# Two more weight-block sums of each seven-product pair made by adding DMAs, with the first two sums' signs turned

## The chip, the cores and the metric

The kernel runs on one core of a Trainium2 chip. The metric is the device time of one execution in microseconds; a version's time is the median of its runs. A profiled execution gives the trace, whose times count from the first instruction.

## The reference

A trunk of two layers on 256 positions with a model width of 2048, all in fp32. The first layer is a gated MLP whose positions are mixed in chunks of 128, the second is stick-breaking attention with 16 heads of 128. Each layer normalizes its input, multiplies it with a wide weight matrix, mixes, gates, and multiplies with an output matrix; the result is added to the residual.

```python
def reference(x, norm_g, a_w_in, a_v_norm_g, a_w_s, a_b_s, a_w_out, b_w_in, b_w_out, final_g):
    h = x
    for i in range(DEPTH):
        hn = rms_norm(h, norm_g[i])
        j = i // N_MIXERS
        if i % N_MIXERS == 0:
            y = gmlp_branch(hn, a_w_in[j], a_v_norm_g[j], a_w_s[j], a_b_s[j], a_w_out[j])
        else:
            y = stick_breaking_branch(hn, b_w_in[j], b_w_out[j])
        h = h + y
    return rms_norm(h, final_g)
...
def gmlp_branch(xn, w_in, v_g, w_s, b_s, w_out):
    proj = xn @ w_in                       # 2048 x 12288: u | v | gate
    ...
    y = u * mixed * jax.nn.silu(zg)
    return y @ w_out                       # 4096 x 2048
...
def stick_breaking_branch(xn, w_in, w_out):
    proj = xn @ w_in                       # 2048 x 8192: q | k | v | gate
    ...
    o = o.reshape(B, S, SB_WIDTH) * jax.nn.silu(zg)
    return o @ w_out                       # 2048 x 2048
```

## The kernel before

**Splitting.** Each fp32 operand is split into a high part `hi` and a remainder `lo`, and a product is made of three matmuls (`terms`, lines 119 to 121: hi·hi, lo·hi, hi·lo). For weights this is done by `cut` (lines 114 and 115): ScalarE casts a block of 128x1024 into `hi`, VectorE subtracts to make `lo`. Five pairs of such buffers exist (`wspl`), so the splitting can run ahead of TensorE by five blocks.

**Pairs.** The weights are read in column blocks of 512 (`CB`). Two column blocks are worked on together, as a `Pair`. There are 22 pairs in the program: three of the v projection (named v2, v4, v6 after their column block), eight gu (gate and u of one block), two o, four qk, two bv, two bg, and one f2. For a part of the rows (`HALVES`, four or five row blocks of 128 in each half, `ks`) the pair uses a scheme of seven block products in place of eight (Strassen's, in a form of Winograd's). The left operand is split into two position tiles (`a11`, `a12` belong to the first 128 positions, `a21`, `a22` to the second), the right operand into blocks `b11`, `b12`, `b21`, `b22` (first digit: half of the rows, second digit: column block). It needs four sums of the left side (s1 to s4: made once for each operand by `Left.sums`, `fifth` or `sums_of`) and four sums of weight blocks, made for each pair:

- b12 - b11, multiplied with s1 (product p5)
- b22 + (b12 - b11), multiplied with s2 (p6)
- b12 + b22, multiplied with s3 (p7)
- b21 less the second sum, multiplied with a22 (p4)

Every group of two row blocks is one tile of 128x1024 (0.524 MB); with five row blocks there is a third group of one row block, 128x512. Groups 0 and 1 live in `sraw`, one buffer for each of the eight tags; a third group of b21 and b22 is loaded into `wraw` by `others`.

**How the sums are made before.** In `head`, b11 is multiplied (p1), then `minus` (lines 284 to 286) overwrites b11 with b12 - b11 on VectorE, and `plus` (lines 288 to 294) lets an adding DMA, issued by POOL, add block (1, 1), which is b22, into b12. After p5, line 314 adds b22 into b11 on VectorE for the groups 0 and 1; a third group gets its addition from an adding DMA. In `body`, p6 uses b11; p2 uses b21; p7 uses b12; then line 339 calls `minus` once more for b21 - b11 into b11, for all groups; p3 uses b22 and p4 uses b11.

**Order.** The bank `a` holds p1, then also p2; `e` holds p5. A copy of `e` in SBUF (`es`, line 328) is added to the banks `b` (line 334) and `c` (line 342). After p4 come `mid` (the pair's own work: gains or position mixing) and `column(0)`: the remaining rows, in raw blocks of two row blocks, three buffers (`wraw`), multiplied in the plain way. `column(1)` is kept back as `tail` and its steps are put between the blocks of the next pair's p1, p5 and p6 (`run`).

**Queues.** SyncE issues the plain loads (line 223). POOL issues the adding DMAs; their list is `adds`. The loads of the gains `vg` (line 527) and of the mixing matrices `ws` (line 597) are issued by POOL after `adds[-1]`, the last add so far; `ws` then gets a triangular selection on POOL (line 602), a cast on ScalarE (line 604) and a subtract on VectorE (line 605). Each engine works through its own queue in order; the order within it is laid down when the program is built, by a simulated timeline and a few ordering constraints.

Of the kernel before, what the change touches and what calls it, by code (L numbers as in the profile page):

```python
# [11 lines left out]
AF = mybir.ActivationFunctionType  # L12
# [17 lines left out]
def trunk_kernel(ctx: ExitStack, tc: tile.TileContext, x, xt, gcols, wst, a_w_in, a_v_norm_g,  # L30
# [11 lines left out]
    nc = tc.nc  # L42
# [45 lines left out]
    def f(ap):  # L88
        return ap.bitcast(F32)
# [33 lines left out]
    class Left:  # L123
# [10 lines left out]
        def sums(self, ks, out, name):  # L134

            for k0 in range(0, ks, 4):
                n = min(4, ks - k0)
                full = []
                for i in range(2):
                    sl = slice(i * ks + k0, i * ks + k0 + n)  # L140
                    fl = sraw.tile([P, 4, S], F32, tag=f"b1{i + 1}_1", name=f"{name}_full{i}{k0}")
                    nc.vector.tensor_add(fl[:, 0:n], f(self.hi[:, sl, :]), f(self.lo[:, sl, :]))
                    full.append(fl)
                a11, a12 = full[0][:, 0:n, 0:P], full[1][:, 0:n, 0:P]
                a21, a22 = full[0][:, 0:n, P:S], full[1][:, 0:n, P:S]
                sm = [sraw.tile([P, 2, 4, P], F32, tag=f"b2{i + 1}_1", name=f"{name}_sm{i}{k0}") for i in range(2)]
                s1, s2, s3, s4 = sm[0][:, 0, 0:n], sm[0][:, 1, 0:n], sm[1][:, 0, 0:n], sm[1][:, 1, 0:n]
                nc.vector.tensor_sub(s1, a21, a22)
                nc.vector.tensor_sub(s3, a21, a11)
                nc.vector.tensor_sub(s2, a11, s1)  # L150
                nc.vector.tensor_sub(s4, a12, s2)
                for i, si in enumerate((s1, s2, s3, s4)):
                    o = out[:, :, i, k0:k0 + n]
                    nc.scalar.copy(o[:, 0], si)
                    nc.vector.tensor_sub(o[:, 1], si, f(o[:, 0]))
            self.s, self.ks = [out], ks

        def fifth(self, out, name):

            full = jk.tile([P, 2, S], F32, tag="sg0", bufs=1, name=f"{name}_full")  # L160
            sm = jk.tile([P, 4, P], F32, tag="sg1", bufs=1, name=f"{name}_sm")
            for i in range(2):
                for t in range(NT):
                    hi, lo = self.part(HALVES[i][4], t)
                    nc.vector.tensor_add(full[:, i, t * P:(t + 1) * P], f(hi), f(lo))
            a11, a12, a21, a22 = full[:, 0, 0:P], full[:, 1, 0:P], full[:, 0, P:S], full[:, 1, P:S]
            nc.vector.tensor_sub(sm[:, 0], a21, a22)
            nc.vector.tensor_sub(sm[:, 1], a11, sm[:, 0])
            nc.vector.tensor_sub(sm[:, 2], a21, a11)
            nc.vector.tensor_sub(sm[:, 3], a12, sm[:, 1])  # L170
            nc.scalar.copy(out[:, 0, :, 0], sm)
            nc.vector.tensor_sub(out[:, 1, :, 0], sm, f(out[:, 0, :, 0]))
            self.s.append(out)

        def sums_of(self, y, ks, out, name):

            a11, a12 = y[0][:, :, 0:P], y[1][:, :, 0:P]
            a21, a22 = y[0][:, :, P:S], y[1][:, :, P:S]
            s13, s24 = (jk.tile([P, ks, P], F32, tag=f"sg{i}", bufs=1, name=f"{name}_{i}") for i in range(2))

            def split(i, si):
                o = out[:, :, i, 0:ks]
                nc.scalar.copy(o[:, 0], si)
                nc.vector.tensor_sub(o[:, 1], si, f(o[:, 0]))
            nc.vector.tensor_sub(s13, a21, a22)
            nc.vector.tensor_sub(s24, a11, s13)
            split(0, s13)
            split(1, s24)
            nc.vector.tensor_sub(s13, a21, a11)
            nc.vector.tensor_sub(s24, a12, s24)  # L190
            split(2, s13)
            split(3, s24)
            self.s, self.ks = [out], ks
# [39 lines left out]
    class Pair:  # L233
# [47 lines left out]
                tick(1)  # L281
                yield

        def minus(self, into, b0, b1, order=None):
            for g in order or range(len(self.groups)):
                nc.vector.tensor_sub(into[g], b0[g], b1[g])  # L286

        def plus(self, into, i, j, g0=0):

            for g in self.early:  # L290
                if g < g0:
                    continue
                k, n = self.groups[g]
                adds.append(nc.gpsimd.dma_start(into[g], self.src(HALVES[i][k], n, j), accum_op=ALU.add))  # L294

        def head(self):
            left = self.left
            self.b11 = self.load(0, 0)
            late = chain and self.name == "v2"
            if not late:  # L300
                self.b12 = self.load(0, 1)
            self.a = self.bank("a")
            for g, _ in enumerate(self.block(self.b11, lambda k: left.part(HALVES[0][k], 0), self.a, "p1", True)):
                yield
                if late and g == 0:
                    self.b12 = self.load(0, 1)
            self.b22 = self.load(1, 1)
            self.minus(self.b11, self.b12, self.b11, self.early)
            self.plus(self.b12, 1, 1)
            self.e = self.bank("e")  # L310
            yield from self.block(self.b11, lambda k: left.sum_part(0, k), self.e, "p5", True)
            self.b21 = self.load(1, 0)
            for g in range(len(self.b22)):
                nc.vector.tensor_add(self.b11[g], self.b22[g], self.b11[g])  # L314
            self.plus(self.b11, 1, 1, len(self.b22))

        def body(self, between=lambda: None):
            left = self.left
            b11, b12, b22, b21 = self.b11, self.b12, self.b22, self.b21

            def block(*args):
                for _ in self.block(*args):
                    between()
            a, e = self.a, self.e
            b = self.bank("b")
            nc.scalar.copy(b, a)
            es = jk.tile([P, CB], F32, tag="es", bufs=1, name=f"{self.name}_es")
            nc.scalar.copy(es, e)
            block(b11, lambda k: left.sum_part(1, k), b, "p6")
            c = self.bank("c")  # L330
            nc.scalar.copy(c, b)
            self.others(b21, 0)
            block(b21, lambda k: left.part(HALVES[1][k], 0), a, "p2")
            self.last_dve = nc.vector.tensor_add(b, b, es)
            self.others(b22, 1)
            block(b12, lambda k: left.sum_part(2, k), c, "p7")
            d = self.bank("d")
            self.last_act = nc.scalar.copy(d, c)
            self.minus(b11, b21, b11)
            block(b22, lambda k: left.sum_part(3, k), b, "p3")  # L340
            block(b11, lambda k: left.part(HALVES[1][k], 1), d, "p4")
            nc.vector.tensor_add(c, c, es)
            self.banks = ((a, d), (b, c))
            if self.mid is not None:
                self.mid(self)
            for _ in self.column(0):
                pass
# [239 lines left out]
    with ExitStack() as lg:  # L587
# [35 lines left out]
        def evac_gu(b, j, t, bank):  # L623
            y = v_of(t, b * CB, CB)
            sg = jk.tile([P, CB], F32, tag=f"sg{t}", bufs=1, name=f"{'gu'[j]}{b}_{t}")
            nc.scalar.activation(sg, bank, (AF.Silu, AF.Gelu_apprx_tanh)[j], scale=r1[:, t:t + 1])
            if j == 0:
                nc.vector.tensor_mul(y, y, sg)
            else:

                queue.append((1, lambda: times(y, sg)))

        def mid_gu(b, pair):
            nonlocal rv
            if rv is None:
                rv = rstd(1, NV, W, "nv")
                for i in (NV - 2, NV - 1):
                    gain(i, pair)
            mixing(b, pair)
            if b == NV - 1:  # L640
                drain()
                flush(make_yTs(0, "xs", "yc0"))
                for k2 in (12, 13):
                    make_yT(k2, yc3(k2))

        for b in range(NV):
            run(Pair(columns(a_w_in, 2 * W + b * CB, b * CB), left, KD, f"gu{b}", KS_GU[b],
                     lambda j, t, bank, b=b: evac_gu(b, j, t, bank), mid=lambda pair, b=b: mid_gu(b, pair), fifth_first=True))
# [120 lines left out]
    def plain(c, ks, before=None):  # L769
        return product(block_of(a_w_out, c * CB, CB), yl0, ks, f"op{c}", lambda t, bank: add_h(c, t, bank), before)  # L770
# [22 lines left out]
    g = plain(0, rest[16:20] + rest[:16] + rest[20:], beside_o0)  # L793
# [9 lines left out]
    g = plain(1, rest)  # L803
# [388 lines left out]
```

## Time and profile before

| what | value |
|---|---|
| median of 3 runs | 1144.99 us (1144.73 to 1146.62) |
| profiled execution, first to last instruction | 1142.0 us |
| its own time outside that span | not recorded; the median stands 3.0 us above the span |
| mean granted TensorE clock | 0.999 |
| TensorE busy | 1132.3 us (99%) |
| VectorE busy | 1010.9 us (89%) |
| ScalarE busy | 828.5 us (73%) |
| POOL busy | 99.8 us (9%) |
| moved by DMA | 264.72 MB, mean 232 GB/s |
| DMA issues by SyncE's and ScalarE's queues, share of 16 engines | 58.9% and 0.8% |
| DMA issues by POOL, share of 16 engines | 16.2% |

How to read the views: in the timeline a row has its start and its duration in us, the engine, the line, the operation, and out<-in by the program's names (without the number of the pair or the buffer). In brackets stands how long the engine was idle before it, and what ended that. L12 is line 12 of the kernel before. In a window's row stand the window and its length, each engine's busy time with its number of instructions, the granted clock, the mean busy share of the 16 DMA engines and the rate. Packets of different queues overlap, so that this share can pass 1. In the list of waits stand the time in all, how often, and the longest.

### The profile page before, as it was taken

What the parts mean: (1) busy time and instruction counts of PE and PEld (TensorE: products, weight loads), DVE (VectorE), ACT (ScalarE), POOL (GpSimd) and SP (SyncE); (2) the same over time, 40 slices, a digit from 0 to 9 for tenths busy, and PEclk for the clock granted to TensorE, in tenths of its full rate; (3) what the DMA queues carried; (4) which work ended last, traced back from release to release, by engine and by line L of the source; (5) the groups of instructions that cost most, each with busy time, mean ns of one, the idle gap of its engine ahead of it and who ended that gap; (6) DMA issues with size and microseconds to landing.
All of it is one profiled execution on the core that took longest, in us unless ns stands there. A gap on an engine that the chain in (4) does not pass through costs nothing.

```text
span 1142.0 us, 14838 instructions
## 1 busy us (share of the span) xinstructions
PE 1132.3 (99%) x5168; PEld 937.6 (82%) x5168; DVE 1010.9 (89%) x1111; ACT 828.5 (73%) x1102; POOL 99.8 (9%) x106
## 2 busy tenths in 40 slices
PE   9999999999999999999999999999999999999997
PEld 6788888888888888888888888888888888888886
DVE  7899889988998999978988678989889989897996
ACT  8776777777777778866657456788678887886564
POOL 0100110110110210100010001110100101100000
PEclk9999999999999999999999999999999999999999
DMA  9988788787797797685885868687687776837972
GB/s 335 317 290 270 214 252 270 194 266 241 173 274 249 191 261 240 177 296 142 267 259 166 276 203 282 153 280 211 181 283 200 211 230 174 272 88 241 325 225 92
DMA packets 135659, 264.72 MB, mean 232 GB/s; under 512 B 8992, under 2 KB 9504, under 8 KB 135456
## 3 DMA queue, kind: packets, MB, share of 16 engines
q1 hardware_dynamic: 117472, 227.57, 58.9%
q0 software_dynamic: 16304, 33.04, 16.2%
q10 hardware_dynamic: 1808, 3.17, 0.8%
q8 instruction: 40, 0.66, 0.2%
q14 instruction: 35, 0.29, 0.1%
HBM read 259.55 MB, written 4.19 MB: 231 GB/s over the span
## 4 chain that ended last, share of the span: by engine, by line
PE 93%; DMA 2%; DVE 2%; issue 1%; ACT 1%; SPq 0%; POOLq 0%; POOL 0%; ACTq 0%; DVEq 0%
PE gu_a L119 3%; PE gu_b L119 3%; PE gu_b L121 3%; PE gu_a L121 3%; PE gu_a L120 3%; PE gu_b L120 3%; PE op_acc L119 2%; PE op_acc L120 2%; PE op_acc L121 2%; PE gu_d L119 2%; PE gu_d L121 2%; PE gu_c L121 2%; PE gu_d L120 2%; PE gu_c L119 2%; PE gu_c L120 2%; PE qk_a L121 1%
## 5 line engine op out<-in xcount | busy, mean ns | idle before, releaser
L114 ACT CAST gu_p_hi<-gu_b 128x1024 fp32r<-128x1024 f32 (+1 forms) x126 | 122.9, 1004 | 38.4 <-DVE gu_b L314 16.1
L115 DVE TENSOR_TENSOR gu_p_lo<-gu_b,gu_p_hi 128x1024 fp32r<-128x1024 f32 (+1 forms) x126 | 142.8, 1165 | 1.9 <-ACT gu_p_hi L114 1.2
L115 DVE TENSOR_TENSOR qk_p_lo<-qk_b,qk_p_hi 128x1024 fp32r<-128x1024 f32 (+1 forms) x77 | 80.8, 1073 | 8.9 <-ACT qk_p_hi L114 8.4
L114 ACT CAST qk_p_hi<-qk_b 128x1024 fp32r<-128x1024 f32 (+1 forms) x77 | 70.5, 934 | 19.0 <-DMA qk_b<-in_b_w_in 4.0
L115 DVE TENSOR_TENSOR gu_lo<-gu_raw,gu_hi 128x1024 fp32r<-128x1024 f32 x60 | 72.1, 1218 | 12.5 <-ACT gu_hi L114 12.2
L114 ACT CAST gu_hi<-gu_raw 128x1024 fp32r<-128x1024 f32 x60 | 62.0, 1052 | 21.0 <-DMA gu_raw<-in_a_w_in 11.5
L115 DVE TENSOR_TENSOR v_lo<-v_raw,v_hi 128x1024 fp32r<-128x1024 f32 (+1 forms) x41 | 48.9, 1193 | 15.2 <-ACT v_hi L114 15.2
L114 ACT CAST v_hi<-v_raw 128x1024 fp32r<-128x1024 f32 (+1 forms) x41 | 41.7, 1028 | 27.9 <-DMA v_raw<-in_a_w_in 26.4
L115 DVE TENSOR_TENSOR v_p_lo<-v_b,v_p_hi 128x1024 fp32r<-128x1024 f32 x42 | 50.3, 1220 | 3.3 <-ACT v_p_hi L114 3.1
L114 ACT CAST v_p_hi<-v_b 128x1024 fp32r<-128x1024 f32 x42 | 43.0, 1049 | 9.8 <-PE v_c L121 4.9
L115 DVE TENSOR_TENSOR bg_p_lo<-bg_b,bg_p_hi 128x1024 fp32r<-128x1024 f32 (+1 forms) x42 | 42.5, 1041 | 4.8 <-ACT bg_p_hi L114 4.7
L114 ACT CAST o_p_hi<-o_b 128x1024 fp32r<-128x1024 f32 (+1 forms) x35 | 33.4, 965 | 18.1 <-PE op_acc L121 13.0
L115 DVE TENSOR_TENSOR bv_p_lo<-bv_b,bv_p_hi 128x1024 fp32r<-128x1024 f32 (+1 forms) x42 | 42.5, 1040 | 3.8 <-ACT bv_p_hi L114 3.6
L114 ACT CAST bv_p_hi<-bv_b 128x1024 fp32r<-128x1024 f32 (+1 forms) x42 | 37.4, 908 | 10.0 <-DMA bv_b<-in_b_w_in 3.0
L294 POOL DMA_DIRECT2D gu_b<-in_a_w_in x20 | 23.0, 1155 | 240.2 <-DVE gu_b L286 134.3
L114 ACT CAST bg_p_hi<-bg_b 128x1024 fp32r<-128x1024 f32 (+1 forms) x42 | 37.3, 907 | 8.0 <-PE bg_a L121 2.5
L115 DVE TENSOR_TENSOR o_p_lo<-o_b,o_p_hi 128x1024 fp32r<-128x1024 f32 (+1 forms) x35 | 38.3, 1113 | 5.4 <-ACT o_p_hi L114 5.4
L286 DVE TENSOR_TENSOR gu_b<-gu_b,gu_b 128x1024 f32<-128x1024 f32 (+1 forms) x36 | 41.4, 1169 | 0.1
L114 ACT CAST o_hi<-o_raw 128x1024 fp32r<-128x1024 f32 x22 | 23.0, 1052 | 24.9 <-DMA o_raw<-in_a_w_out 24.8
L115 DVE TENSOR_TENSOR o_lo<-o_raw,o_hi 128x1024 fp32r<-128x1024 f32 x22 | 26.7, 1221 | 15.2 <-ACT o_hi L114 15.0
L114 ACT CAST op_hi<-op_raw 128x1024 fp32r<-128x1024 f32 x24 | 25.1, 1053 | 19.3 <-PE op_acc L121 8.8
L120 PE MATMUL op_acc<-op_lo,yc 128*128 128x512 f32 x96 | 37.8, 393 | 0.0
(798 smaller groups left out, 3797.8 us busy)
## 6 DMA issues: line engine op xcount, KB each, us to landing
gu_b<-in_a_w_in SPq DMA_DIRECT2D x64, 512.0 KB, 4.8
gu_raw<-in_a_w_in SPq DMA_DIRECT2D x60, 512.0 KB, 5.4
v_raw<-in_a_w_in SPq DMA_DIRECT2D x39, 512.0 KB, 5.5
qk_b<-in_b_w_in SPq DMA_DIRECT2D x32, 512.0 KB, 5.3
qk_raw<-in_b_w_in SPq DMA_DIRECT2D x26, 512.0 KB, 5.5
v_b<-in_a_w_in SPq DMA_DIRECT2D x24, 512.0 KB, 5.4
op_raw<-in_a_w_out SPq DMA_DIRECT2D x24, 512.0 KB, 4.9
o_raw<-in_a_w_out SPq DMA_DIRECT2D x22, 512.0 KB, 4.7
```

The lines of the kernel that those rows point to most:

```text
L114: nc.scalar.copy(hi[:, sl], raw[:, sl])
L115: low[0] = nc.vector.tensor_sub(lo[:, sl], raw[:, sl], f(hi[:, sl]))
L119: nc.tensor.matmul(acc, lh, hi, start=first, stop=False, skip_group_check=True)
L120: nc.tensor.matmul(acc, lh, lo, start=False, stop=False, skip_group_check=True)
L121: nc.tensor.matmul(acc, ll, hi, start=False, stop=last, skip_group_check=True)
L286: nc.vector.tensor_sub(into[g], b0[g], b1[g])
L294: adds.append(nc.gpsimd.dma_start(into[g], self.src(HALVES[i][k], n, j), accum_op=ALU.add))
```

## The change

Four things are changed, in all 22 pairs.

- The sum for p4: for the groups 0 and 1, `minus(b11, b21, b11)` on VectorE is gone. In its place, directly after p6, POOL issues `plus(b11, 1, 0, 0, 2)`: an adding DMA reads block (1, 0), which is b21, from HBM once more and adds it into b11. A third group keeps its subtract on VectorE.
- So that b21 only has to be added, the first two sums of the groups 0 and 1 are kept with the other sign: b11 gets b11 - b12 (a third group b12 - b11 as before), and line 314 subtracts b22 where it added it.
- The left sums match: in `sums` and `sums_of` s2 is turned (s1 - a11, and s4 = a12 + s2); in `fifth`, which serves the third group, s1 is turned (a22 - a21, and s2 = a11 + s1).
- p5 then comes out with the other sign, and the copy of `e` into `es` becomes an activation with scale -1.

The new adds are appended to `adds` as well, so that `vg` and `ws` are issued after them.

```diff
@@ Left.sums @@
-                nc.vector.tensor_sub(s2, a11, s1)
-                nc.vector.tensor_sub(s4, a12, s2)
+                nc.vector.tensor_sub(s2, s1, a11)
+                nc.vector.tensor_add(s4, a12, s2)
@@ Left.fifth @@
-            nc.vector.tensor_sub(sm[:, 0], a21, a22)
-            nc.vector.tensor_sub(sm[:, 1], a11, sm[:, 0])
+            nc.vector.tensor_sub(sm[:, 0], a22, a21)
+            nc.vector.tensor_add(sm[:, 1], a11, sm[:, 0])
@@ Left.sums_of @@
-            nc.vector.tensor_sub(s24, a11, s13)
+            nc.vector.tensor_sub(s24, s13, a11)
...
-            nc.vector.tensor_sub(s24, a12, s24)
+            nc.vector.tensor_add(s24, a12, s24)
@@ Pair @@
-        def minus(self, into, b0, b1, order=None):
-            for g in order or range(len(self.groups)):
-                nc.vector.tensor_sub(into[g], b0[g], b1[g])
-
-        def plus(self, into, i, j, g0=0):
+        def plus(self, into, i, j, g0=0, g1=9):
 
             for g in self.early:
-                if g < g0:
+                if not g0 <= g < g1:
                     continue
@@ head @@
-            self.minus(self.b11, self.b12, self.b11, self.early)
+            for g in self.early:
+                b = (self.b11[g], self.b12[g])[::1 if g < 2 else -1]
+                nc.vector.tensor_sub(self.b11[g], *b)
...
-                nc.vector.tensor_add(self.b11[g], self.b22[g], self.b11[g])
+                nc.vector.tensor_sub(self.b11[g], self.b11[g], self.b22[g])
@@ body @@
-            nc.scalar.copy(es, e)
+            nc.scalar.activation(es, e, AF.Identity, scale=-1.0)
             block(b11, lambda k: left.sum_part(1, k), b, "p6")
+            self.plus(b11, 1, 0, 0, 2)
...
-            self.minus(b11, b21, b11)
+            for g in range(2, len(self.groups)):
+                nc.vector.tensor_sub(b11[g], b21[g], b11[g])
```

## The prediction

> **What bounds the kernel now.** I read the page's busy times first, then the waits of TensorE, then windows over the span, and last the timeline of the first pair.
>
> ```profile
> span 1142.0 us, 14838 instructions
> PE 1132.3 (99%) x5168; PEld 937.6 (82%) x5168; DVE 1010.9 (89%) x1111; ACT 828.5 (73%) x1102; POOL 99.8 (9%) x106
> ```
>
> A busy TensorE isn't proof of one at its full rate, so the next two views are needed: what it waited for in the whole span, and how many matmuls it got through in windows with much and with little other work.
>
> ```profile
> PE wps L79 <- DVE warm L76: 1.3, 1, 1.3
> PE v_acc L120 <- DVE v_lo L115: 0.6, 1, 0.6
> PE gT L434 <- ACT bsg L1011: 0.2, 1, 0.2
> PE v_acc L119 <- ACT v_hi L114: 0.2, 1, 0.2
> ...
> 20.00:40.00 20.00, 19.44 (x86) 1.00 0.93 321
> 40.00:60.00 20.00, 20.00 (x90) 1.00 1.07 340
> 60.00:80.00 20.00, 19.86 (x88) 1.00 0.91 314
> 600.00:620.00 20.00, 20.00 (x94) 1.00 0.50 155
> 1080.00:1100.00 20.00, 20.00 (x90) 1.00 0.98 297
> 1120.00:1140.00 20.00, 14.76 (x66) 0.99 0.26 96
> ```
>
> Four waits, 2.3 us in all, three of them in the first 40 us (the loads and the first product, where the change does nothing). The windows (length, TensorE busy and its instructions, granted clock, DMA share, GB/s) show 90 matmuls in 20 us at a DMA share of 1.07 and 90 at 0.98; the 94 of the window with 0.50 hold short transposes. The clock is granted in full. So the rate of a matmul depends on nothing beside it, and from 40 us to the last product the only losses are the 0.14 us missing in 60:80 and the 0.2 us before gT. The change alters no matmul. TensorE sets the end, and what can be won is 0.34 us; the 7.2 us that it lacks in the last window and behind it belong to the final norm and the stores.
>
> **The change part by part.**
>
> (1) Removed: two subtracts into b11 in each pair (the groups 0 and 1; a group 2 keeps its own). One row holds all of line 286, then the queues' shares:
>
> ```profile
> 0.00:1142.00 1142.00, 120.52 (x110) 1.00 0.76 232
> q1 hardware_dynamic: 117472, 227.57, 58.9%
> q0 software_dynamic: 16304, 33.04, 16.2%
> ```
>
> 22 pairs run (v 3, gu 8, o 2, qk 4, bv 2, bg 2, f 1), so 44 of the 110 go, all of 128x1024. With 22 narrow ones at 0.68 us taken off, the 88 wide ones take 1.20 us each: 53 us leave VectorE, which falls from 1010.9 to some 958 us. That is worth the part of TensorE's waiting that VectorE caused after 40 us, which is none recorded. Its margin was thin in places:
>
> ```profile
> 438.24 3.48 DVE L115 TENSOR_TENSOR gu_p_lo<-gu_b,gu_p_hi 128x1024 fp32r<-128x1024 f32 x3
> 439.62 0.40 PE L120 MATMUL gu_b<-gu_p_lo,xs 128*128 128x512 f32 x1
> ```
>
> The first of the three subtracts ends near 439.45 and TensorE takes its result at 439.62. The change widens a margin of 0.17 us, but a margin isn't time: I count 0 us.
>
> (2) Added: 44 adding DMAs of 0.524 MB on POOL's queue, 23.1 MB. The software queue's 33.04 MB cost 16.2% of 1142 us, 185 us of all 16 engines, so 5.6 us per MB; the plain queue's 227.57 MB cost 673 us, 3.0 us per MB. The new work is 129 us, the share of the DMA engines rises from 0.76 to 0.87, and one pair gets 1.05 MB, 5.9 us. Whether that matters is read stage by stage. In a steady pair (gu1, the adds would run from about 217 to 227):
>
> ```profile
> 216.00:228.00 12.00, 12.00 (x55) 9.93 (x54) 11.72 (x12) 10.66 (x13) 1.14 (x1) 1.00 0.59 181
> 228.00:240.00 12.00, 12.00 (x55) 9.93 (x54) 9.10 (x11) 8.35 (x12) 0.00 (x0) 1.00 1.00 355
> 240.63 1.22 DVE L115 TENSOR_TENSOR gu_lo<-gu_raw,gu_hi 128x1024 fp32r<-128x1024 f32 x1
> 245.59 0.39 PE L120 MATMUL gu_a<-gu_lo,x_hi 128*128 128x512 f32 x1
> ```
>
> (Length, busy time of TensorE, of its weight loads, of VectorE, ScalarE and POOL, then clock, DMA share, GB/s.) From 216 to 228 the DMA engines are free for 0.41 x 12 = 4.9 us of the 5.9 needed. The last 1.0 us is pushed into the full stretch behind it. The raw block that is loaded at the end of that stretch is split by 241.85 and used at 245.59, a margin of 3.7 us that covers it: 0 us. With the cover gone, what the push has over 3.7 us would be lost in each such pair, at most 5.9 - 3.7 = 2.2 us, which only a hole filled by something else could bring about. I keep 0.7 us in all for the upper end.
>
> In the first pair (v2) there is no such hole:
>
> ```profile
> 12.00:16.00 4.00, 4.00 (x19) 3.06 (x18) 3.95 (x8) 4.00 (x9) 0.00 (x0) 1.00 1.04 409
> 52.00:56.00 4.00, 4.00 (x19) 3.32 (x18) 3.94 (x5) 2.48 (x3) 0.00 (x0) 1.00 1.10 262
> 60.00:76.00 16.00, 15.86 (x70) 12.82 (x69) 13.64 (x15) 10.49 (x15) 0.00 (x0) 1.00 1.00 349
> 76.00:80.00 4.00, 4.00 (x19) 3.30 (x19) 3.75 (x4) 3.87 (x5) 0.00 (x0) 1.00 0.57 175
> ```
>
> The engines are busy without a break to 76 us. Room there is only the difference of rates: 349 GB/s from 60 to 76 against the best plain 409, 15% of 16 us, 2.3 us. So of 5.9 us some 3.6 us push the loads behind them. Which load is late first:
>
> ```profile
> 75.17 1.05 ACT L114 CAST v_hi<-v_raw 128x1024 fp32r<-128x1024 f32 x1 [5.51 <-DMA v_raw<-in_a_w_in]
> 76.25 1.23 DVE L115 TENSOR_TENSOR v_lo<-v_raw,v_hi 128x1024 fp32r<-128x1024 f32 x1 [2.34 <-ACT v_hi L114]
> 79.67 0.39 PE L120 MATMUL v_a<-v_lo,x_hi 128*128 128x512 f32 x1
> ```
>
> This raw block waited for its buffer and then for its load; its lo is ready at 77.48 and used at 79.67, a margin of 2.2 us. A push of 3.6 us makes a stall of 1.4 us, which nothing later gives back. Bounds: below, a push under 2.2 us, stall 0; above, all 5.9 us, stall 3.7 us. I take 1.4 us because the rate between 60 and 76 us is a measured room and not a guess.
>
> The Trainium skill ("DMA: Bandwidth & Descriptors", Where 436 GB/s comes from) puts the ceiling of the 16 ports at 435 GB/s; this case's best window moved 409. With its figure the room would be an estimated 3.2 us, the push 2.7, and the stall 0.5 us; by the measured 409 it is 1.4 us, and I keep the measurement.
>
> (3) The new wait. The adds can start when the blocks of p6 have been split, and p4 now waits for their landing. Queued behind them on POOL are the vg and ws loads, which are issued after the last add of the pair.
>
> ```profile
> 53.18 2.50 DVE L115 TENSOR_TENSOR v_p_lo<-v_b,v_p_hi 128x1024 fp32r<-128x1024 f32 x2
> v_b<-in_a_w_in POOLq DMA_DIRECT2D x2, 512.0 KB, 10.7
> 65.24 1.06 ACT L114 CAST v_p_hi<-v_b 128x1024 fp32r<-128x1024 f32 x1
> 69.92 0.39 PE L120 MATMUL v_d<-v_p_lo,x_hi 128*128 128x512 f32 x1
> ```
>
> p6's second split ends at 55.7; with the 10.7 us that the two adds of this stage took to land it is there at 66.4, 1.2 us behind the cast of 65.24. With 1.06 and 1.22 us for the two splits, lo is ready at 68.7, and TensorE needs it at 69.92: 0 us, with 1.2 us to spare; should they take 4 us longer, 2.8 us, but that comes from the same crowd of transfers as (2), and of the two only the later stall counts. In gu1:
>
> ```profile
> 215.66 2.50 DVE L115 TENSOR_TENSOR gu_p_lo<-gu_b,gu_p_hi 128x1024 fp32r<-128x1024 f32 x2
> gu_b<-in_a_w_in POOLq DMA_DIRECT2D x16, 512.0 KB, 7.0
> 228.79 1.06 ACT L114 CAST gu_p_hi<-gu_b 128x1024 fp32r<-128x1024 f32 x1 [0.17 <-PE gu_c L121]
> 230.63 0.41 ACT L604 CAST wh<-ws 128x256 fp32r<-128x256 f32 x1
> ws<-in_wst POOLq DMA_DIRECT2D x8, 128.0 KB, 7.9
> ```
>
> The splits end at 218.2; plus 7.0 is 225.2, before the casts of p4 around 228.8, 0 us. ws is issued behind both adds, near 219.4, lands near 227.3, and has 3.3 us before its cast for a selection of about one us: 0 us. vg feeds only products on VectorE that are queued between splits; late, it would delay them by less than the margin, 0 us.
>
> (4) Moved and equal: signs of s1 to s4, the alternating operands of the first sum and the add that becomes a subtract keep their count and shape, 0 us. The copy into es becomes an activation with a scale. Nearest rows: 585 ns for the copy, 684 ns for an Identity out of PSUM:
>
> ```profile
> L621 ACT ACTIVATE v<-mix,cols 128x512 f32<-128x512 f32 x16 | 10.2, 684 | 15.4 <-PE mix L619 15.4
> L328 ACT COPY gu_es<-gu_e 128x512 f32<-128x512 f32 x8 | 4.7, 585 | 0.5 <-PE gu_e L121 0.5
> ```
>
> 0.1 us x 22 on ScalarE, which is 73% busy: 0 us, at most 0.1 us in v2.
>
> Sum: 1142.0 + 1.4 = 1143.4 us of the profiled execution. The median of the three runs, 1144.99, stands 3.0 us above that span (what lies around it, and the spread between runs of 1.9 us); I carry the 1.4 us over: 1146.4 us.
>
> **The rivals.**
> - Hidden altogether: ACT and VectorE run earlier in v2, loads spread, the push stays under 2.2 us. For it: the share passes 1.0 without harm in 40:60. Time 1145.0.
> - Slower, the other side: the adds in v2 push the loads by more than 4.5 us, from where the stall passes 2.3 us. For it: 52:56 moved only 262 GB/s while two such adds were in flight. At the full 5.9 us: 1144.99 + 3.7 = 1148.7. Against it: the following window at 0.57 catches up.
> - Late landings in steady pairs: p4 waits for the adds in each of the 11 pairs of four blocks, where p4 follows p6 soonest. In gu1 10.6 us lie between p6's split (218.2) and p4's cast (228.79), and the adds took 7.0, so they would have to take 3.6 us longer before even the cast moves. Every 0.3 us lost beyond that in each of the 11 costs 3.3 us: 1144.99 + 3.3 = 1148.3.
> - Faster: VectorE at 89% as a hidden limit. All that it could return after 40 us is 0.34 us, 1144.7, which isn't outside no change. To gain more, matmuls would have to come closer together, and the windows speak against that.
> - Descriptor starvation: POOL cannot write its list while VectorE holds something that both need, so each add starts up to one subtract later. Two starts, 2 x 1.2 us, turn the 1.2 us to spare in v2 into a stall of 1.2 us on top: 1147.6. The Trainium skill ("SBUF — State Buffer", the two separate sides) says that an fp32 copy of VectorE locks POOL out so. Against it, the 66 adds issued here took POOL 72.95 us, 1.1 us each, beside a VectorE at 89%:
>
> ```profile
> 0.00:1142.00 1142.00, 72.95 (x66) 1.00 0.76 232
> ```
>
> **How the numbers follow.** A measurement of this kernel tells about 0.2%, 2.3 us, from no change. Stall of 0.5 to 2.3 us in v2 0.36 (forecast); hidden 0.28; push over 4.5 us 0.22; late landings 0.06; starvation 0.04, slower by 2.6 us; faster beyond 2.3 us 0.04 for something that the profile doesn't show. Same 0.36 + 0.28 = 0.64, slower 0.32, faster 0.04. The range runs from the hidden case less the spread below the median and the 0.34 us, 1144.2, to the full push with 0.7 us for (2)'s steady pairs, 1149.4.
>
> **What would show it.** Right: line 286 at 66 instructions, VectorE near 958 us, DMA near 288 MB and 0.87, 110 adds, no wait of TensorE after 100 us, and between 60 and 85 us a wait for a raw block's split of one to two us. Wrong: TensorE waiting in gu or bg pairs for a split of b11 (late landings), POOL's issues well over 1.1 us (starvation), or TensorE without any wait after 40 us (hidden).

## The result, and the profile after

The changed kernel takes 1152.95 us in the median of 6 runs (1150.02 to 1153.88), the kernel before 1146.13 us beside it (6 runs, 1144.73 to 1149.59). The ratio is 1.0057 with a 95% interval of 1.0039 to 1.0074: slower by about 6.5 us, where 1146.4 us and a range up to 1149.4 us had been forecast.

The page of the changed kernel, first the lines of the span, of the engines and of the two large DMA queues:

```profile
span 1150.5 us, 14914 instructions
PE 1136.8 (99%) x5168; PEld 935.6 (81%) x5168; DVE 964.2 (84%) x1067; ACT 825.4 (72%) x1102; POOL 154.0 (13%) x150
DMA packets 147627, 287.79 MB, mean 250 GB/s; under 512 B 9696, under 2 KB 10208, under 8 KB 147424
q1 hardware_dynamic: 117472, 227.57, 57.2%
q0 software_dynamic: 28272, 56.11, 28.0%
PE 83%; DMA 7%; DVE 4%; ACT 3%; issue 2%; POOL 0%; SPq 0%; POOLq 0%; ACTq 0%; DVEq 0%
```

Everything that was to be moved has moved: VectorE has 44 instructions fewer and falls from 1010.9 to 964.2 us, and POOL's queue moves 23.1 MB more. The last line is the chain of work that ended last: DMA, which hardly stood in it before, now has 7%. Where TensorE waits, its list says (total, count, longest):

```profile
PE v_d L119 <- ACT v_d L337: 0.9, 1, 0.9
PE v_acc L120 <- DVE v_lo L115: 0.9, 2, 0.7
PE gu_c L119 <- ACT gu_c L330: 0.6, 1, 0.6
PE v_a L119 <- ACT v_p_hi L114: 0.4, 2, 0.2
PE qk_d L119 <- ACT qk_d L337: 0.3, 1, 0.3
PE mix L617 <- ACT wh L604: 0.3, 1, 0.3
```

Only v_acc belongs to the first 40 us; the other waits weren't there before. (Not shown are two more rows of the first 40 us, 1.3 and 1.1 us, and three of 0.2 us.) The windows of 20 us (length, TensorE, its loads, VectorE, ScalarE, POOL, clock, DMA share, GB/s) place the loss; in the kernel before the first of them holds 88 matmuls and the others 90 each:

```profile
60.00:80.00 20.00, 19.11 (x85) 15.51 (x84) 13.59 (x14) 10.38 (x16) 0.00 (x0) 1.00 1.06 348
80.00:100.00 20.00, 19.78 (x87) 15.84 (x86) 18.89 (x17) 16.12 (x21) 4.41 (x5) 1.00 0.77 198
120.00:140.00 20.00, 19.75 (x86) 15.65 (x85) 17.18 (x16) 14.35 (x19) 2.81 (x3) 1.00 0.78 196
160.00:180.00 20.00, 19.79 (x86) 15.74 (x85) 15.63 (x22) 13.39 (x18) 2.46 (x2) 1.00 0.75 203
180.00:200.00 20.00, 19.09 (x82) 14.91 (x82) 17.98 (x20) 16.10 (x24) 5.36 (x7) 1.00 0.96 274
```

A wait costs TensorE some 0.1 us more than its own length, since the first matmul behind it is slow to start (0.50 us in place of 0.39 behind the 0.9). So I put both traces side by side, matmul by matmul in the order of time, and take how much later the matmul of the same number starts than before: the lag. (From 86 us on some matmuls stand in another order; in the changed kernel 665 of the 5168 numbers hold another product.) The columns are the time in the kernel before, and the rows all kernels of this study, one trace each (us later than before):

```
before at        61    74   115   124   158   169   183   206   233   677   888  1096  1119
changed         1.4   2.1   2.8   3.7   3.7   4.5   4.5   6.6   6.6   7.1   7.7   7.8   8.5
signs_only      1.0   0.6   0.6   0.6   0.6   0.6   0.6   0.6   0.6   2.0   2.0   5.8   5.8
early_four      0.6   1.2   1.9   2.9   2.9   3.4   3.4   5.4   5.8   5.8   5.8   7.5   7.7
later_eighteen  1.0   0.5   0.5   0.5   0.5   0.5   0.5   0.6   0.6   0.7   0.7   0.7   0.7
ghost_three    -0.1  -0.3   1.9   5.7   5.7   6.0   6.0  11.3  11.3  11.6  11.6  11.6  12.0
early_three     1.6   2.1   2.8   4.0   4.0   4.4   4.4  11.3  11.3  12.2  12.4  13.9  14.6
gu0_only        0.6   1.2   1.2   1.2   1.2   1.2   1.2   1.4   1.4   1.4   1.4   1.7   2.1
eighth_four     0.4  -0.1  -0.1  -0.1  -0.1  -0.1  -0.1   2.0   2.0   2.0   2.0   2.5   2.8
three_pause     0.6   1.5   2.3   3.3   3.3   3.6   3.6   5.5   5.5   6.3   6.3   6.3   6.3
copy_first     -0.2   0.2   2.4   3.3   3.3   3.6   3.6   5.8   5.8   6.9   6.9   9.0   9.7
fourth_raw      1.6   2.2   2.2   2.2   2.2   2.2   2.2   4.3   4.3   4.3   5.1   6.3   6.3
power_first     0.5   1.6   1.6   1.6   1.6   1.6   1.6   1.6   1.6   1.6   1.6   1.6   2.8
mended          1.2   0.9   0.9   1.2   1.2   1.2   1.2   1.2   1.2   1.2   1.5   1.5   1.5
```

The changed kernel loses time at five places. From the finer steps: p4 of v2 (1.2 us; just ahead of it 0.5 us of the lag goes, which the kernel before lost there), the raw block behind v2 (0.7), behind v4 (0.9), behind v6 (0.8), and gu0 (2.1): 5.2 us in all between 61 and 206 us. At the raw blocks the list of waits has only 0.2 us each, because the loss is spread over several late starts: behind v2 four matmuls from 81.08 on start 0.33, 0.61, 0.34 and 0.30 us behind one another in place of 0.23. What lies ahead of 61 us, and the small steps of the long rest, differ by a few us between single traces of any two kernels (signs_only has 5.2 us behind 233 us, later_eighteen 0.1) and are given to no cause.

What ScalarE does at four of these places in the changed kernel (in brackets the idle time before, and what ended it):

```profile
68.48 1.05 ACT L114 CAST v_p_hi<-v_b 128x1024 fp32r<-128x1024 f32 x1 [2.54 <-DMA v_b<-in_a_w_in]
69.43 0.58 ACT L337 COPY v_d<-v_c 128x512 f32<-128x512 f32 x1
...
79.96 1.05 ACT L114 CAST v_hi<-v_raw 128x1024 fp32r<-128x1024 f32 x1 [7.07 <-DMA v_raw<-in_a_w_in]
...
121.67 1.05 ACT L114 CAST v_hi<-v_raw 128x1024 fp32r<-128x1024 f32 x1 [8.73 <-DMA v_raw<-in_a_w_in]
...
163.29 1.05 ACT L114 CAST v_hi<-v_raw 128x1024 fp32r<-128x1024 f32 x1 [8.41 <-DMA v_raw<-in_a_w_in]
```

At 68.48 the cast of p4's second block waits for its adding DMA, and the copy of bank c into d stands behind it in ScalarE's queue. The product p3 doesn't need this copy, but p4's very first matmul does: TensorE waits 0.9 us for the copy, not for a split. The other three are the fourth raw block of `column(0)`. SyncE issues its load behind the eight `b` loads of the next pair, and only when one of the three raw buffers is free. Behind v2 the chain of work shows how p4's late add reaches it (start, length):

```profile
56.55 11.83 DMA v_b<-in_a_w_in
...
71.31 1.23 DVE v_lo L115
72.55 7.32 DMA v_raw<-in_a_w_in
```

On VectorE the split of p4's late block holds up the split of the first raw block (71.31); the end of that split frees a buffer, and the load goes out at 72.55. Before, it went out at 69.86 and took 5.2 us. So the cast is 4.8 us later (79.96 against 75.17): 1.4 us are lag from ahead of the adds, 1.3 us the buffer, and 2.1 us the slower landing. Plain loads have become slower in general. Issues with the median time to landing, before and after (the first two rows are of the kernel before):

```profile
v_b<-in_a_w_in SPq DMA_DIRECT2D x24, 512.0 KB, 5.4
gu_b<-in_a_w_in SPq DMA_DIRECT2D x64, 512.0 KB, 4.8
...
v_b<-in_a_w_in SPq DMA_DIRECT2D x24, 512.0 KB, 9.0
gu_b<-in_a_w_in SPq DMA_DIRECT2D x64, 512.0 KB, 6.9
v_b<-in_a_w_in POOLq DMA_DIRECT2D x12, 512.0 KB, 9.1
```

### The profile page after: what moved, and what is told of

The parts are those of the page before. It is cut to its first block, busy times and chain, and to the rows that moved or that the text cites. A ratio compares the mean times of both kernels' runs of the same rounds, so it can differ in the third digit from the quotient of the medians.

```text
span 1150.5 us, 14914 instructions
## 1 busy us (share of the span) xinstructions
PE 1136.8 (99%) x5168; PEld 935.6 (81%) x5168; DVE 964.2 (84%) x1067; ACT 825.4 (72%) x1102; POOL 154.0 (13%) x150
## 4 chain that ended last, share of the span: by engine, by line
PE 83%; DMA 7%; DVE 4%; ACT 3%; issue 2%; POOL 0%; SPq 0%; POOLq 0%; ACTq 0%; DVEq 0%
DMA v_raw<-in_a_w_in 3%; PE gu_b L119 2%; PE gu_b L120 2%; PE gu_b L121 2%; PE gu_a L120 2%; PE gu_a L121 2%; PE gu_a L119 2%; PE op_acc L119 2%; PE op_acc L121 2%; PE op_acc L120 2%; PE gu_c L120 2%; PE gu_c L119 2%; PE gu_c L121 2%; PE gu_d L120 2%; PE gu_d L121 2%
## 5 line engine op out<-in xcount | busy, mean ns | idle before, releaser
L290 POOL DMA_DIRECT2D gu_b<-in_a_w_in x36 | 42.1, 1173 | 230.5 <-DVE gu_b L306 99.5
L290 POOL DMA_DIRECT2D qk_b<-in_b_w_in x22 | 24.8, 1163 | 199.8 <-DVE qk_b L306 91.3
L115 DVE TENSOR_TENSOR qk_lo<-qk_raw,qk_hi 128x1024 fp32r<-128x1024 f32 x26 | 31.3, 1219 | 8.2 <-ACT qk_hi L114 8.1
```

Of the source, the lines that this page charges most:

```text
L115: low[0] = nc.vector.tensor_sub(lo[:, sl], raw[:, sl], f(hi[:, sl]))
```

## The experiments

Three groups of four kernels were run, each group on one chip beside the kernel before (medians there 1146.58, 1145.86 and 1145.12 us). Across groups, ratios are compared.

| kernel | median, us | ratio to before, 95% interval |
|---|---|---|
| signs_only | 1145.75 | 0.9989 (0.9975 to 1.0004) |
| early_four | 1152.89 | 1.0046 (1.0031 to 1.0062) |
| later_eighteen | 1144.90 | 0.9985 (0.9971 to 0.9999) |
| ghost_three | 1156.66 | 1.0077 (1.0051 to 1.0102) |
| early_three | 1157.17 | 1.0097 (1.0082 to 1.0111) |
| gu0_only | 1146.05 | 0.9999 (0.9988 to 1.0010) |
| eighth_four | 1147.45 | 1.0012 (1.0001 to 1.0024) |
| fourth_raw | 1149.57 | 1.0032 (1.0023 to 1.0041) |
| three_pause | 1150.98 | 1.0042 (1.0027 to 1.0057) |
| copy_first | 1153.43 | 1.0066 (1.0051 to 1.0081) |
| power_first | 1146.07 | 1.0003 (0.9989 to 1.0018) |
| mended | 1145.89 | 1.0002 (0.9993 to 1.0011) |

### Which part, and which pairs

The first three and two later ones choose in which pairs the sum is made by DMA; elsewhere VectorE makes it, with the turned signs kept everywhere:

```diff
-            self.plus(b11, 1, 0, 0, 2)
+            by_dma = False        # signs_only
+            #  self.name in ("v2", "v4", "v6", "gu0")        early_four
+            #  self.name not in ("v2", "v4", "v6", "gu0")    later_eighteen
+            #  self.name in ("v2", "v4", "v6")               early_three
+            #  self.name == "gu0"                            gu0_only
+            if by_dma:
+                self.plus(b11, 1, 0, 0, 2)
...
+                elif not by_dma:
+                    nc.vector.tensor_add(b11[g], b21[g], b11[g])
```

> All signs turned as in the change, but the last sum of the groups 0 and 1 is added by VectorE, so that no DMA is added. Two theories name the new DMAs: crowding (the adds take transfer time in the first four pairs, where raw blocks have little margin) and waiting (p4's split waits for the landing, and what is queued behind it on ScalarE waits too). Both expect the time of before: ratio 1.000, between 0.998 and 1.002, VectorE near 1011 us, no wait of TensorE after 40 us over 0.3 us. The rival, that the turned signs or the order of instructions that was laid down with them cost the time, expects 1.006.

Measured: 0.9989, no difference. The signs, the activation into `es` and the order that follows from them cost nothing.

> Adding DMAs for the last sum in v2, v4, v6 and gu0 alone, VectorE adds in the other 18 pairs. In the changed kernel TensorE lost 0.9 us at p4 of v2, 0.8 to 0.9 us at the first raw blocks behind each of v2, v4 and v6, and 2.0 us in gu0, 5.3 us in all. Crowding and waiting both place these there: ratio 1.004 to 1.005. If the loss were spread over all adds, 4 of 22 pairs would cost about 1.3 us: 1.001.

Measured: 1.0046, most of the loss of all 22 pairs, with the steps of the changed kernel at the same places (the lag grows from 0.6 at 61 us to 5.4 at 206).

> The reverse: adding DMAs for the last sum in the 18 pairs from gu1 on, VectorE adds in v2, v4, v6 and gu0. My theory: these pairs have holes in the transfers and margins of over 3 us, so only the 2.0 us go that the changed kernel lost behind 210 us: ratio 1.000 to 1.002. If the loss were spread over all adds: 1.005.

Measured: 0.9985, at the edge of what can be told from no change; 36 of the 44 adds are free. The lag stays at 0.5 to 0.7 us from 74 us to the end.

> Adds made by DMA only in the pairs v2, v4 and v6; VectorE makes the sum with b21 everywhere else, gu0 included. If the stalls behind v2, v4 and v6 belong to these pairs' own adds, 0.9 us at v2's p4 and 0.8, 0.9 and 0.8 us at the raw blocks behind the three pairs come back, 3.4 us, ratio to before 1.003, and gu0 shows none of its 2 us. Rival: gu0's stall is the late end of the crowding in the v pairs; then gu0 loses its 2 us here as well, 5.4 us, ratio 1.0047.

> Adds made by DMA only in gu0. If gu0's stall comes from its own two adds, it loses 2 us between 190 and 210 us and nothing before, ratio 1.0017. Rival (crowding carried over from the v pairs): no loss, ratio 1.000.

Measured: gu0's adds alone cost nothing (0.9999), so gu0's stall isn't made by its own adds, as the rival had it. But without them, behind v pairs that run late, gu0 loses more and not less: 6.9 us between 183 and 206 us, ratio 1.0097. Neither theory had that. It became the question of three_pause below.

### What of an add costs: the wait or the bytes

ghost_three lets VectorE make every sum; in v2, v4 and v6 the same two adding DMAs go into two spare blocks that nobody reads, each behind a one-element copy from p6's split:

```diff
+            if self.name in ("v2", "v4", "v6"):
+                for g in range(2):
+                    nc.vector.tensor_copy(scrap[g][:, 0, 0:1], f(self.los[g][:, 0, 0:1]))
+                    k, n = self.groups[g]
+                    adds.append(nc.gpsimd.dma_start(scrap[g], self.src(HALVES[1][k], n, 0), accum_op=ALU.add))
```

> VectorE makes the last sum everywhere, with the signs turned. In v2, v4 and v6 the same adding DMAs run at the same place (behind a one-element copy from p6's second split), but into two spare blocks that nobody reads. That separates the transfers from the wait. Crowding: TensorE still loses 0.8 us or so at the first raw blocks behind each of the three pairs, 2 to 3 us in all, ratio 1.002, and none at p4 of v2. Waiting: nothing is lost, 1.000.

Measured: 1.0077. The crowding theory had the places right and the size wrong, 1.002. With nobody waiting for the adds, p4 of v2 has no stall (lag -0.1 to -0.3), and the raw blocks behind v2 and v4 cost more than in the changed kernel (2.2 and 3.8 us; of the 3.8, some 1.9 us are matmuls at half speed behind the wait, as the last section tells). Behind v2 the load goes out at 69.62, as in the kernel before, and lands 9.3 us later in place of 5.2: the crowd of transfers alone is enough. Another 5.3 us are lost in gu0, where TensorE waits 2.9 us for `vh`, which stands behind the power `nv_r` (6.03 us there). VectorE keeps its work here as well, so the sizes aren't those of the change.

eighth_four keeps number, place and waits of the adds in v2, v4, v6 and gu0, but each covers 64 of the 512 columns; VectorE adds the others, and makes the whole sums in the later pairs:

```diff
+            by_dma = 64 if self.name in ("v2", "v4", "v6", "gu0") else 0
...
+                adds.append(nc.gpsimd.dma_start(b11[g][:, :, 0:by_dma], self.src(HALVES[1][k], n, 0)[:, :, 0:by_dma], accum_op=ALU.add))
...
+                    nc.vector.tensor_add(b11[g][:, :, by_dma:], b21[g][:, :, by_dma:], b11[g][:, :, by_dma:])
```

> In v2, v4, v6 and gu0 the same number of adding DMAs, with the same waits at the same places, but over 64 of the 512 columns of each block only; VectorE makes the other columns' sums, and the whole sums in the later pairs. If the bytes that the adds move crowd out the plain loads, an eighth of them leaves at most 0.5 us, ratio 1.000 to 1.0005. Rival (each add costs a fixed time on its queue or by the wait for its landing, whatever its size): the loss of the four pairs stays, ratio 1.004 to 1.005.

Measured: 1.0012, above the 1.0005 expected. In the v pairs an eighth of the bytes takes the whole loss away (the lag is -0.1 us from 74 to 183 us), so it is bytes and not the number of adds. But gu0 loses 2.1 us here too, in a single wait of TensorE, for the copy into bank d:

```profile
PE gu_d L119 <- ACT gu_d L340: 1.8, 1, 1.8
...
187.47 0.44 POOL L608 TENSOR_SCALAR_AFFINE_SELECT ws<-ws 128x256 f32<-128x256 f32 x1 [6.62 <-DMA ws<-in_wst]
187.90 1.68 POOL L97 TENSOR_TENSOR nv_r<-nv_ms,half 128x2 f32<-128x2 f32 x1
189.61 1.34 ACT L616 ACTIVATE vh<-v,nv_r 128x512 fp32r<-128x512 f32 x2 [2.46 <-POOL nv_r L97]
190.85 1.03 ACT L114 CAST gu_p_hi<-gu_b 128x1024 fp32r<-128x1024 f32 x1
191.79 0.57 ACT L340 COPY gu_d<-gu_c 128x512 f32<-128x512 f32 x1
```

(The first line is from TensorE's waits, the others from the timelines of POOL and ScalarE.) This is gu0's own trap: `nv_r`, the power behind the norm of v (line 97, only two elements per partition), was placed behind the selection of `ws` in POOL's queue, and so behind the late load of `ws`; `vh`, a cast of p4 and the copy into d follow it on ScalarE. In the changed kernel and gu0_only the power stands ahead of the selection.

### Why gu0 lost more without its adds

In early_three the power isn't behind a late load. It starts right after its input and takes 3.9 us. POOL, then VectorE, and ScalarE behind them:

```profile
192.20 3.89 POOL L97 TENSOR_TENSOR nv_r<-nv_ms,half 128x2 f32<-128x2 f32 x1 [6.46 <-DVE nv_ms L95]
...
191.96 0.15 DVE L95 TENSOR_SCALAR nv_ms<-nv_tot 128x2 f32<-128x2 f32 x1
192.02 3.48 DVE L115 TENSOR_TENSOR gu_p_lo<-gu_b,gu_p_hi 128x1024 fp32r<-128x1024 f32 x3
...
196.12 1.33 ACT L615 ACTIVATE vh<-v,nv_r 128x512 fp32r<-128x512 f32 x2 [3.03 <-POOL nv_r L97]
197.37 1.03 ACT L114 CAST gu_p_hi<-gu_b 128x1024 fp32r<-128x1024 f32 x1
198.30 0.57 ACT L339 COPY gu_d<-gu_c 128x512 f32<-128x512 f32 x1
```

The power ends at 196.09, 0.6 us behind the last of three splits that VectorE ran without a pause. three_pause is early_three with one instruction more, which makes VectorE wait for the power after the first of these splits:

```diff
         nc.gpsimd.tensor_tensor(r, ms, half, op=ALU.pow)
+        if name == "nv":
+            seen = const.tile([P, NT], F32, name=f"{name}_seen")
+            nc.vector.tensor_copy(seen, r)
```

> The kernel with adds in v2, v4 and v6 only lost 6.1 us in gu0, where it has no adds at all. Theory: GpSimd's small power (nv_r, 128x2, 0.7 us elsewhere) took 3.9 us because it got no turn while VectorE ran three splits back to back, and the casts of vh and of p4 and the copy into bank d stand behind it on ScalarE. Here VectorE copies nv_r (128x2) after one of these splits, so it must pause until the power is done; nothing else changes. Expected: the power under 2 us, the loss in gu0 under 1 us, 1157.2 down to 1151.7, ratio to before 1.005. Rival (gu0's blocks land late, the power is late with them): the pause changes nothing or costs 0.5 us, ratio 1.010.

```profile
191.45 1.62 POOL L97 TENSOR_TENSOR nv_r<-nv_ms,half 128x2 f32<-128x2 f32 x1 [5.33 <-DVE nv_ms L95]
```

Measured: the power takes 1.62 us in place of 3.89, and the time falls from 1.0097 to 1.0042; gu0 loses 1.9 us and not 6.9. The theory holds: a wait put into VectorE's queue made the kernel 6 us faster. What is left in gu0 is more than the 1 us expected and comes in small steps, splits and casts that run late behind v6's late raw block.

### The mends

copy_first: the changed kernel, with v2's copy into d ahead of the cast of p4's second block.

```diff
-                hi, lo = cut(b[g], n, f"{self.name}_{nm}{g}")
+                with tc.issue_after(ins_of(self.last_act)) if (self.name, nm, g) == ("v2", "p4", 1) else ExitStack():
+                    hi, lo = cut(b[g], n, f"{self.name}_{nm}{g}")
```

> The changed kernel, but in v2 the copy into bank d is put ahead of the cast of p4's second block on ScalarE. The wait at p4 (0.9 us) should go. If it and the wait for the raw block behind it come from one crowd of transfers, the raw block's stall takes it over (0.8 becomes 1.7 us) and the time stays: ratio 1.0057. Rival (two separate losses): 0.9 us less, ratio 1.005. The place of TensorE's loss up to 85 us tells them apart, the time alone hardly.

```profile
65.81 0.57 ACT L338 COPY v_d<-v_c 128x512 f32<-128x512 f32 x1 [0.25 <-PE v_c L121]
67.47 1.05 ACT L114 CAST v_p_hi<-v_b 128x1024 fp32r<-128x1024 f32 x1 [1.10 <-DMA v_b<-in_a_w_in]
...
79.60 1.04 ACT L114 CAST v_hi<-v_raw 128x1024 fp32r<-128x1024 f32 x1 [8.23 <-DMA v_raw<-in_a_w_in]
```

Measured: 1.0066, no gain. The wait at p4 is gone (0.2 us of lag at 74 us), and the raw block behind v2 takes it over: 2.2 us there. The two waits of v2 are one loss, and whichever is mended alone hands it to the other.

fourth_raw: the changed kernel, with a buffer of its own for the fourth raw block in v2, v4 and v6, loaded ahead of the next pair's eight `b` loads.

```diff
-                raw = wraw.tile([P, 2, CB], F32, tag="raw", name=f"{self.name}_{j}{ks[0]}_raw")
+                if j == 0 and i == 6 and self.name in ("v2", "v4", "v6"):
+                    raw = extra[0].tile([P, 2, CB], F32, tag=f"raw4_{self.name}", name=f"{self.name}_{j}{ks[0]}_raw")
+                else:
+                    raw = wraw.tile([P, 2, CB], F32, tag="raw", name=f"{self.name}_{j}{ks[0]}_raw")
...
-                    load(raw, self.src(ks[0], 2, j))
+                    load(raw, self.src(ks[0], 2, j), behind=j == 0 and i == 6 and self.name in ("v2", "v4", "v6"))
```

> The changed kernel, all 44 adds, but in v2, v4 and v6 the fourth raw block of the first column has a buffer of its own and is loaded ahead of the next pair's eight b loads. If the stalls behind these three pairs come from this block being the last in a queue that the adds have slowed, they go (0.8 + 0.9 + 0.8 us) while v2's p4 (0.9 us) and gu0 (2 us) stay: about 2.5 us less than the changed kernel, ratio to before 1.003 to 1.004. Rival (the engines simply have too much to move up to 200 us, whatever the order): another block is late instead, ratio stays at 1.0057.

Measured: 1.0032, as expected: no loss at all from 74 to 183 us with the same bytes to move. So the bytes make the loads late, but whether that costs anything hangs on one load in each of the three pairs. The edit gives it both a buffer of its own and an earlier place (in v2 it goes out at 53.30 in place of 72.55); the two weren't tried apart. In gu0 the order laid down at build time now has the power behind the selection, and the same wait of 1.8 us as in eighth_four stands there.

power_first: fourth_raw, with `nv_r` ahead of the selection on POOL. mended: that, and copy_first's edit.

```diff
-            with tc.issue_after(ins_of(pair.last_act)), tc.issue_after(ins_of(pair.last_dve)):
+            with tc.issue_after(ins_of(pair.last_act)), tc.issue_after(ins_of(rpow['nv'] if b == 0 else pair.last_dve)):
                 nc.gpsimd.affine_select(ws, ws, pattern=[[0, GPB], [1, P]], compare_op=ALU.is_ge, fill=0.0,
```

> The changed kernel with the fourth raw block ahead in v2, v4 and v6, and in gu0 the small power nv_r put ahead of the triangular selection of ws on GpSimd, which waits for a load that lands late. If the 1.8-us wait for the copy into bank d in gu0 comes from that order, it goes: ratio 1.0032 becomes 1.0016 (the 0.9 us of v2's p4 and small steps stay). Rival: ws itself or the next blocks are as late, TensorE waits there instead, ratio 1.003.

> All three mends in the changed kernel: the fourth raw block ahead, the power ahead of the selection, v2's copy into bank d ahead of p4's second cast. If the loss of the change is these late loads at places with thin margins, little is left of it: no wait over 0.3 us between 40 and 240 us, ratio 1.000 to 1.001. Rival (44 more adding DMAs cost TensorE time of their own, by slower matmuls or elsewhere): 1.003 or more.

Measured: 1.0003 and 1.0002. In power_first gu0 loses nothing and only p4 of v2 is left (1.1 us), less than the 1.0016 expected, which the interval still holds. Since the power stands there as in the changed kernel, ahead of the selection, gu0's loss in the changed kernel came from the late raw blocks of the v pairs. In mended TensorE waits for nothing between 40 and 220 us. Windows of mended, with the columns as above:

```profile
60.00:80.00 20.00, 20.00 (x89) 16.33 (x88) 15.34 (x16) 12.27 (x17) 0.00 (x0) 1.00 1.07 342
80.00:100.00 20.00, 20.00 (x90) 16.57 (x89) 18.70 (x16) 15.71 (x23) 5.87 (x6) 1.00 0.89 246
120.00:140.00 20.00, 20.00 (x90) 16.57 (x89) 17.16 (x15) 15.16 (x20) 6.01 (x6) 1.00 0.86 220
160.00:180.00 20.00, 20.00 (x90) 16.57 (x89) 17.84 (x21) 14.95 (x20) 6.12 (x7) 1.00 0.75 178
180.00:200.00 20.00, 20.00 (x90) 16.57 (x89) 17.92 (x22) 16.21 (x24) 1.71 (x3) 1.00 1.04 331
```

With all 44 adds the kernel is as fast as before, to 0.1%. The loss was a matter of order and of one spare buffer at a few places, and mending them brings no gain over before. The only version whose whole interval lies ahead of the kernel before is later_eighteen, and by a hair (0.9971 to 0.9999).

## Why the prediction was wrong, point by point

**Right: TensorE sets the end and VectorE's 53 us are worth nothing.** VectorE fell to 964 us (958 forecast), and no version gained more than 0.15%, mended with 964.8 us of VectorE nothing at all. Signs and `es` cost nothing (signs_only).

**Right: the price of the adds.** 5.6 us per MB had been taken. POOL's queue went from 185.0 to 322.1 us of all engines (28.0% of 1150.5) for 23.1 MB more: 5.9 us per MB. The DMA share is 0.86 (0.87 forecast).

**Right in mechanism, and in size partly by luck: v2.** A push of 3.6 us was to make the raw block behind v2 late, with a stall of 1.4 us. The push was 3.4 us (4.8 less the 1.4 of lag from ahead of the adds), and v2 in all lost 1.4 us (lag 1.4 at 61 us, 2.8 at 115). But the block itself cost only 0.7; the rest came from p4, where nothing had been forecast, less the 0.5 us that came back. copy_first shows that both belong to one push, 2.2 us when the block takes it alone.

**Wrong, step (3): "0 us, with 1.2 us to spare" for p4's wait in v2.** I asked whether the split would be ready, and forgot what is queued behind the waiting cast: the copy into d, which p4's first matmul needs. Both stood in the kernel before:

```profile
66.19 0.59 ACT L338 COPY v_d<-v_c 128x512 f32<-128x512 f32 x1
68.11 0.39 PE L119 MATMUL v_d<-v_p_hi,x_hi 128*128 128x512 f32 x1
```

With the forecast landing at 66.4, the cast of 1.06 and the copy of 0.59 us end near 68.05: 0.1 us to spare, and not 1.2. And 10.7 us is the median of two adds that took 9.4 and 12.1; p4's last block waits for the later one, which took 11.8 us here. TensorE waited 0.9 us.

**Wrong, step (2): "0 us" for the steady pairs, the larger miss (3.8 us).** The margin of 3.7 us and the hole of 4.9 us were read in gu1 and carried to pairs with neither. v4 and v6 read as follows in the kernel before (the split of the raw block, and the matmul that takes it):

```profile
117.72 1.23 DVE L115 TENSOR_TENSOR v_lo<-v_raw,v_hi 128x1024 fp32r<-128x1024 f32 x1 [3.75 <-ACT v_hi L114]
120.47 0.39 PE L120 MATMUL v_a<-v_lo,x_hi 128*128 128x512 f32 x1
...
157.44 1.23 DVE L115 TENSOR_TENSOR v_lo<-v_raw,v_hi 128x1024 fp32r<-128x1024 f32 x1 [2.68 <-ACT v_hi L114]
161.27 0.39 PE L120 MATMUL v_a<-v_lo,x_hi 128*128 128x512 f32 x1
```

Margins of 120.47 - 118.95 = 1.5 us and 161.27 - 158.67 = 2.6 us. The casts of these blocks, at 116.64 and 156.36 before, came at 121.67 and 163.29: beyond the lag of 2.8 and 3.7 us, a push of 2.2 and 3.2 us. These two rows, not gu1's, were the ones to read: 1.7 us lost there. gu0 comes on top with 2.1 us, for which the step had nothing. Behind v6's late block ScalarE starts on gu0's p6 at 182.13 in place of 175.21, 6.9 us later where TensorE is 4.5 us later. gu0_only shows that gu0's own adds aren't enough, and power_first that without the late raw blocks nothing is lost there. For the later 18 pairs gu1 was a fair sample (later_eighteen).

**The rivals.** "Push over 4.5 us in v2" had the right sign, but its condition wasn't met (3.4 us); the time went at other places. "Late landings" expected p4 to wait in the gu pairs; none of the waits is of that kind but qk_d's 0.3 us. Descriptor starvation did not show: POOL's 110 issues took 125.94 us, 1.14 each, against 1.1 before. But what VectorE holds from POOL did matter elsewhere, at the power `nv_r`, as below.

**Open.** The changed kernel's lag of 1.9 us between 206 us and the end isn't assigned. It lies within what single traces of the other kernels show there.

## What to carry to other kernels

When transfers are added, list the margin of every load that stands last in its queue, pair by pair, from its landing to the instruction that needs it; one steady pair doesn't stand for those before it. For each new wait, read what is queued behind the waiting instruction on the same engine and which buffers come free later by it, and for each tiny instruction on a slow queue, what stands behind it. If a change that should cost nothing costs half a per cent, a few order constraints and a spare buffer may give it back, and moving one load or one small instruction is cheaper to try than undoing the change.

## What the runs showed of the hardware

**A run of splits on VectorE can keep POOL out.** The power on 128x2 takes 0.72 us where VectorE leaves a gap at its start (changed kernel, 191.31), 3.89 us beside three splits in a row, and 6.03 us in ghost_three, where VectorE had no pause from 198.36 to 203.99:

```profile
198.55 6.03 POOL L97 TENSOR_TENSOR nv_r<-nv_ms,half 128x2 f32<-128x2 f32 x1 [5.71 <-DVE nv_ms L95]
```

It ends 0.6 us after VectorE's run does in both. In the kernel before the same power took 1.8 us: it ended 0.6 us after the first split, although the second followed that one without a pause. What decides between the two isn't shown. The Trainium skill ("SBUF — State Buffer", SBUF: two separate sides) says that a VectorE operation with two inputs in SBUF and a GpSimd operation that reads SBUF exclude each other, each for its whole instruction. The traces agree for the power, which in these three runs ends 0.6 us behind a split, and show besides that a run of several such instructions can keep POOL out from end to end. They don't show the other direction for so small an operation: in the changed kernel a split that started 0.02 us behind the power took 1.25 us in place of 1.22.

**After a wait of 1.8 to 2.9 us TensorE can go on at half speed.** In early_three the wait of 2.9 us was followed by a dozen matmuls that start 427 ns apart in place of 227, which with those at both ends of the row cost another 2.9 us; from 198 to 204 us the granted clock is 0.50. The windows of 20 us hold only part of it (columns as above):

```profile
180.00:200.00 20.00, 16.53 (x70) 12.78 (x69) 18.45 (x20) 14.96 (x22) 4.78 (x2) 0.95 0.81 271
200.00:220.00 20.00, 20.00 (x80) 16.32 (x79) 17.42 (x21) 13.67 (x17) 2.29 (x3) 0.88 0.60 172
```

The waits of 1.8 us in eighth_four and fourth_raw weren't followed by it, but one of 1.8 us in ghost_three was. The Trainium skill ("TensorE: Matmul & The Clock Gate", What's actually happening) has the clock halve after an idle window of about 3.4 us that runs free of the kernel; 427 ns agrees with its halved rate, and here shorter waits were enough.
